# 289 products of zero tiles ahead of the first product, with a stationary operand at eleven distances

## The chip, the cores and the metric

The kernel runs on one core of one Trainium2 chip. What is measured is the device time of one execution in microseconds (us). All times below come from the page of one profiled execution, from answers of its trace, or from the timed runs.

## What is computed

Two transformer blocks run one after the other over 256 tokens of 1024 features, in float32. The first block has a SwiGLU feed-forward part, a mixer made of sparse attention and a gated recurrence, and a second feed-forward part; the second block has two layers with feed-forward parts, forgetting attention or latent attention, and a gated per-layer embedding. The part that the change stands ahead of is the very beginning:

```python
def rms_norm(x, g):
    y = xf * lax.rsqrt(jnp.mean(xf * xf, axis=-1, keepdims=True) + EPS)
    return y * g
def swiglu(x, w_gu, w_down):
    gate, up = jnp.split(x @ w_gu, 2, axis=-1)
    return (jax.nn.silu(gate) * up) @ w_down
h = h + 0.5 * swiglu(rms_norm(h, ffn1_norm), ffn1_w_gu, ffn1_w_down)
```

The output is one array of 256 by 1024. None of the products that the change adds is read by anything, so the output is the same.

## The kernel before

The 256 tokens stand in two tiles of 128 (T = 0 and T = 1), and a generator per tile (`net`, stepped in turns by `run`) walks through the whole network. Every weight matrix is cut into units, and these into pieces of at most 128x512 float32. `load_unit` (L301) brings one piece by DMA from the array `wp` into a buffer `wr` (six buffers, L311), and splits it into a rounded high part (ScalarE, L318) and the remainder (VectorE, L319), both in buffers `w` (42 of them, two to a piece). The activations are split the same way into `xh` and `xl`. A product of full accuracy is then three TensorE products, `mm3` at L343:

```python
mm(out, xh, wh, start=start, stop=False)   # L347
mm(out, xh, wl, start=False, stop=False)   # L348
mm(out, xl, wh, start=False, stop=stop)    # L349
```

The first argument after the output is the stationary operand (128 columns), the second the moving one (up to 512 columns). A piece is thus used by three products for T = 0 and three for T = 1.

`build` loads the first unit (`preload(PRE)`), then the constants and the first x tile; then `run` begins. For each token tile `first_xT` (L501) transposes eight blocks of x (`tr`, L357) into two banks of PSUM named `tr` and `mm`, scales them into `xh` on ScalarE (L507) and into `xl` on VectorE (L509). The statistics of the norm go beside it (L527, L448, L454, L493, L494). `late` (L1443) loads the remaining constants, and `gain` (L426) loads a row of 1024 gains or biases into one of three buffers named `gb` (L435).

The order in which each engine takes its instructions is set by the tile scheduler, in program order with priorities; each engine then takes its queue in order. All DMAs are issued by SyncE's one queue (SP). PSUM has per token tile one bank `mm`, one bank `tr` and two banks `a`, the last of which take turns.

Of the kernel before, what the change touches and what calls it, by code (L numbers as in the profile page):

```python
# [11 lines left out]
FT = mybir.dt.float32  # L12
FR = mybir.dt.float32r
# [5 lines left out]
D = 1024  # L19
S = 256  # L20
P = 128
# [242 lines left out]
class Net:  # L264
# [1143 lines left out]
    def run(self):  # L1408
        gens = [self.net(0), self.net(1)]
        done = [False, False]  # L1410
        send = [None, None]
        cnt = [0, 0]

        def step(T):
            if done[T]:
                return
            self.T = T
            try:
                tag = gens[T].send(send[T])
            except StopIteration:  # L1420
                done[T] = True
                return
            send[T] = None
            if tag is not None:
                send[T] = self.get_unit(cnt[T], tag)
                cnt[T] += 1

        step(0)
        self.nc.sync.dma_start(self.x[1], self.a["x"][P:S, :])
        step(1)  # L1430
        steps = [1, 1]
        while not all(done):
            step(0)
            steps[0] += 1
            lag = min(self.lag_at(cnt[0]), LAG0 + steps[0] // RAMP)
            while steps[0] - steps[1] > (lag if not done[0] else 0) and not done[1]:
                step(1)
                steps[1] += 1
                self.drop_units(cnt[1] - 1)
        assert cnt == [len(self.units)] * 2  # L1440


def late(n, nc, sb, a, vec, ct):  # L1443
    nc.sync.dma_start(ct[:, P:a["const"].shape[1]], a["const"][:, P:])
    lf = n.s2()[:, 0:64 * len(LEVELS)]
    nc.sync.dma_start(lf, a["lvl"])
    n.lvl = sb.tile([P, 64 * len(LEVELS)], U8, name="lvl")
    nc.vector.tensor_copy(n.lvl, lf)
    n.c["cpos"] = sb.tile([P, 2, 16], FT, name="cpos")
    nc.sync.dma_start(n.c["cpos"], a["cpos"])  # L1450
    n.w2 = sb.tile([P, 2, 128], FT, name="w2")
    nc.sync.dma_start(n.w2, a["w2"])
    o, w = vec["fox_b_f_2"]
    nc.sync.dma_start(n.bf, a["vec"][o:o + w].rearrange("(o w) -> o w", o=1).broadcast_to([P, w]))
    for k in ("hgrn_out_norm", "kv_norm_2", "mla_q_norm_2"):
        o, w = vec[k]
        n.small[k] = sb.tile([P, w], FT, name=k)
        nc.sync.dma_start(n.small[k], a["vec"][o:o + w].rearrange("(o w) -> o w", o=1).broadcast_to([P, w]))
    n.fsel = n.misc[:, 0:16]
    nc.scalar.activation(n.fsel, n.c["fsel"], AF.Copy)  # L1460


def build(nc, tc, a, units, offs, coff, vec):
    with tc.tile_pool(name="sb", bufs=1) as sb, tc.tile_pool(name="ps", bufs=1, space=PSUM) as ps:
        n = Net(nc, tc, sb, ps, a, units, offs)
        n.vec = vec
        xs = []
        for T in range(2):
            x = sb.tile([P, D], FT, name=f"x{T}")
            xs.append(x)  # L1470
            if T == 0:
                n.preload(PRE)
                nc0 = a["const"].shape[1]
                ct = sb.tile([P, -(-(nc0 + 24) // 32) * 32], FT, name="const")
                nc.sync.dma_start(ct[:, 0:P], a["const"][:, 0:P])
                nc.sync.dma_start(x, a["x"][0:P, :])
                n.c["g1"] = ct[:, nc0:nc0 + 8]
                n.bf = ct[:, nc0 + 8:nc0 + 24]
                nc.sync.dma_start(n.c["g1"], a["g1"])
                n.x, n.small = xs, {}  # L1480
        for k, (o, w) in coff.items():
            n.c[k] = ct[:, o:o + w]
        n.misc = sb.tile([P, 32], FR, name="misc")
        n.c["mhalf"] = n.misc[:, 16:32].bitcast(FT)
        nc.gpsimd.memset(n.c["mhalf"], -0.5)
        n.late = lambda: late(n, nc, sb, a, vec, ct)
        n.run()
# [43 lines left out]
```

## Time and profile before

| what | us |
|---|---|
| timed runs, median of 2 | 1678.89 (1678.06 to 1679.73) |
| the profiled execution, whole | 1682.29 |
| its span, first to last instruction | 1680.5 |
| TensorE products busy in the span | 1649.4 (98%) |
| VectorE busy | 1110.6 (66%) |
| ScalarE busy | 936.7 (56%) |
| mean granted TensorE clock | 0.995 |

In the views, a line names an instruction by the line of the kernel, the engine, the operation and output<-inputs; PE is TensorE's products, PEld its loads of the stationary operand, DVE is VectorE, ACT ScalarE, POOL GpSimd, and SP the queue that issues DMAs. A product's shown duration includes the time that it takes to drain through the array, so that products overlap in the rows: what a product costs in a stream is the distance from its start to the next one's start, and this is what "pace" means below.

### The profile page before, as it was taken

The page shows a single profiled execution, that of the slowest core. Times are in us where ns is not written, and L with a number is a line of the kernel's source. Part 1 is how long each engine was busy: PE and PEld are TensorE (multiplying, and loading weights), DVE is VectorE, ACT ScalarE, POOL GpSimd, SP SyncE. Part 2 cuts the span into 40 slices and gives each one's busy share as a digit, 9 for nine tenths or more (in the row PEclk, how much of TensorE's full clock was granted, in tenths as well). Part 3 has the DMA queues.
Part 4 walks back from the last instruction along what each step waited for, and adds up shares of the span by engine and source line. Part 5 has one row for each costly group of instructions (what it writes and reads, how often), then busy time and mean ns, then how long its engine had stood idle before and what let it go on. Part 6 is the DMA issues. An engine that isn't in the chain of part 4 may idle for free.

```text
span 1680.5 us, 24829 instructions
## 1 busy us (share of the span) xinstructions
PE 1649.4 (98%) x8010; PEld 1345.9 (80%) x8010; DVE 1110.6 (66%) x2308; ACT 936.7 (56%) x1899; POOL 23.5 (1%) x43
## 2 busy tenths in 40 slices
PE   8999999999999999999999999999999999999997
PEld 6888777778888788877888888778888888888886
DVE  7656666666665766677558666785666865766666
ACT  7555665555555555555555555565555775555553
POOL 0000000000000000000000000000000000000000
PEclk9999999999999999999999999999999999999999
DMA  8855554336565566655436555565665633566552
GB/s 280 269 183 174 173 169 127 101 107 194 188 188 176 175 189 189 186 170 151 146 116 206 186 190 188 176 223 171 201 188 165 211 101 94 188 208 187 189 176 76
DMA packets 160403, 293.00 MB, mean 174 GB/s; under 512 B 18192, under 2 KB 27152, under 8 KB 160272
## 3 DMA queue, kind: packets, MB, share of 16 engines
q1 hardware_dynamic: 160272, 291.41, 55.7%
q8 instruction: 63, 1.03, 0.2%
q14 instruction: 68, 0.56, 0.1%
HBM read 290.29 MB, written 1.05 MB: 173 GB/s over the span
## 4 chain that ended last, share of the span: by engine, by line
PE 87%; DVE 6%; ACT 2%; DMA 2%; issue 2%; POOL 1%; SPq 0%; DVEq 0%; POOLq 0%; ACTq 0%
PE mm L347 16%; PE mm L349 15%; PE mm L348 15%; PE a L347 10%; PE a L348 10%; PE a L349 10%; PE tr L357 4%; DMA wr<-wp 1%; DVE w L319 1%; DVE x L542 1%; PE a L766 1%; ACT w L318 1%; DVE x L559 1%; DVE x L547 1%; PE a L989 1%
## 5 line engine op out<-in xcount | busy, mean ns | idle before, releaser
L319 DVE TENSOR_TENSOR w<-wr,w 128x512 fp32r<-128x512 f32 (+3 forms) x1058 | 702.8, 679 | 355.0 <-ACT w L318 171.0
L318 ACT ACTIVATE w<-wr 128x512 fp32r<-128x512 f32 (+3 forms) x1058 | 648.9, 623 | 395.1 <-PE mm L348 235.3
L347 PE MATMUL mm<-w,xh 128*128 128x512 f32 (+3 forms) x1200 | 477.5, 398 | 0.3 <-DVE s L584 0.3
L349 PE MATMUL mm<-w,xl 128*128 128x512 f32 (+3 forms) x1200 | 465.3, 388 | 0.0
L348 PE MATMUL mm<-w,xh 128*128 128x512 f32 (+3 forms) x1200 | 464.7, 387 | 0.0
L347 PEld LDWEIGHTS mm<-w,xh 128*128 128x128 f32 x1200 | 226.0, 188 | 43.9 <-issue 4.4
L349 PEld LDWEIGHTS mm<-w,xl 128*128 128x128 f32 x1200 | 225.9, 188 | 43.3
L348 PEld LDWEIGHTS mm<-w,xh 128*128 128x128 f32 x1200 | 226.6, 189 | 38.9 <-issue 0.6
L347 PE MATMUL a<-w,s 128*128 128x512 f32 x531 | 208.1, 392 | 0.5 <-ACT s L352 0.5
L348 PE MATMUL a<-w,s 128*128 128x512 f32 x531 | 207.5, 391 | 0.0
L349 PE MATMUL a<-w,s 128*128 128x512 f32 x531 | 207.3, 391 | 0.1
L347 PE MATMUL a<-w,xh 128*128 128x512 f32 (+2 forms) x304 | 119.6, 394 | 0.8 <-ACT xh L352 0.7
L347 PEld LDWEIGHTS a<-w,s 128*128 128x128 f32 x531 | 99.7, 188 | 24.9 <-issue 3.6
L348 PE MATMUL a<-w,xh 128*128 128x512 f32 (+2 forms) x304 | 118.3, 389 | 0.0
L349 PE MATMUL a<-w,xl 128*128 128x512 f32 (+2 forms) x304 | 117.2, 388 | 0.0
L349 PEld LDWEIGHTS a<-w,s 128*128 128x128 f32 x531 | 99.6, 188 | 21.1 <-DVE s L353 0.6
L348 PEld LDWEIGHTS a<-w,s 128*128 128x128 f32 x531 | 99.7, 188 | 19.9
L352 ACT ACTIVATE s<-tr 128x256 fp32r<-128x256 f32 (+2 forms) x137 | 50.6, 371 | 70.8 <-PE tr L357 70.7
L353 DVE TENSOR_TENSOR s<-tr,s 128x256 fp32r<-128x256 f32 (+2 forms) x137 | 56.4, 413 | 47.6 <-ACT s L352 47.3
L357 PE MATMUL tr<-const,s 128*128 128x128 f32 (+1 forms) x436 | 77.5, 274 | 1.9 <-DVE s L471 1.5
L357 PEld LDWEIGHTS tr<-const,s 128*128 128x128 f32 (+1 forms) x436 | 55.9, 140 | 27.6 <-DVE s L471 2.7
L347 PEld LDWEIGHTS a<-w,xh 128*128 128x128 f32 x304 | 57.4, 189 | 14.4 <-ACT xh L352 3.3
(277 smaller groups left out, 1354.9 us busy)
## 6 DMA issues: line engine op xcount, KB each, us to landing
wr<-wp SPq DMA_DIRECT2D x994, 256.0 KB, 2.7
gb<-vec SPq DMA_DIRECT2D x21, 512.0 KB, 4.3
wr<-wp SPq DMA_DIRECT2D x32, 192.0 KB, 2.4
w<-wp SPq DMA_DIRECT2D x16, 256.0 KB, 4.6
wr<-wp SPq DMA_DIRECT2D x16, 160.0 KB, 2.4
wr<-wp SPq DMA_DIRECT2D x8, 168.0 KB, 2.2
wr<-wp SPq DMA_DIRECT2D x8, 140.0 KB, 2.3
x<-x SPq DMA_DIRECT2D x2, 512.0 KB, 5.7
```

The lines of the kernel that those rows point to most:

```text
L318: nc.scalar.activation(hi[:, 0:w], r[:, 0:w], AF.Copy)
L319: nc.vector.tensor_tensor(lo[:, 0:w], r[:, 0:w], hi[:, 0:w].bitcast(FT), op=OP.subtract)
L347: mm(out, xh, wh, start=start, stop=False)
L348: mm(out, xh, wl, start=False, stop=False)
L349: mm(out, xl, wh, start=False, stop=stop)
L352: self.nc.scalar.activation(hi, src, AF.Copy)
L353: self.nc.vector.tensor_tensor(lo, src, hi.bitcast(FT), op=OP.subtract)
L357: self.nc.tensor.transpose(out, src, self.c["ident"][0:n, 0:n])
L542: nc.vector.scalar_tensor_tensor(y[:, cs], y[:, cs], nm, g[:, cs], op0=OP.add, op1=OP.mult)
L547: nc.vector.scalar_tensor_tensor(y[:, cs], y[:, cs], r, b[:, cs], op0=OP.mult, op1=OP.add)
L559: self.nc.vector.scalar_tensor_tensor(x[:, cs], acc, c, x[:, cs], op0=OP.mult, op1=OP.add, accum_out=s)
L766: nc.tensor.matmul(hp[0:2 * nb, 256 * kv:256 * kv + 256], kbs[kv][:, cc].rearrange("p g b -> p (g b)"), u[i][0], start=cc == 0, stop=cc == 15)
```

## The change

A function `probe` is called once, for the first token tile, between the loading of the first weight unit and the loading of the constants. It takes two of the three `gb` buffers, fills both with zeros on VectorE, and issues 289 products on TensorE of which nobody reads the result. The moving operand is always the front of one tile; the stationary operand is 128 columns of the other, starting at byte offset f. There are 24 groups: one of 13 products and 23 of 12. By width: 211 products have 512 columns, 78 have 256. Each group takes one of T = 1's two `a` banks in turn.

```diff
+def probe(nc, n):
+    n.T = 1
+    m, w = n.t("gb", [P, D], 3, FR), n.t("gb", [P, D], 3, FR)
+    for v in (m, w):
+        nc.vector.memset(v.bitcast(FT), 0.0)
+    mm = nc.tensor.matmul
+
+    def run(reps, cols, offs):
+        o = n.pt("a")
+        for i in range(reps):
+            c, f = cols[i % len(cols)], offs[i % len(offs)] // 4
+            mm(o[:, 0:c], w[:, f:f + P], m[:, 0:c], start=True, stop=True)
+
+    run(13, [512], [0])
+    for f in (0, 256, 128, 64, 32, 16, 384, 448, 480, 512, 1024):
+        run(12, [512], [f])
+    run(12, [512], [0, 512, 1024])
+    run(12, [512], [0, 256])
+    run(12, [512], [128, 128, 384])
+    for f in (0, 256, 128, 64):
+        run(12, [256], [f])
+    for f in (0, 256, 128, 64):
+        run(12, [512, 256], [f])
+    run(12, [512, 256], [0, 512])
...
                 n.preload(PRE)
+                probe(nc, n)
                 nc0 = a["const"].shape[1]
```

On TensorE, at the start of the program, the order before begins with the eight transposes of the first x tile (`x_61`), seven products of the first token tile, and the eight transposes of the second (`x_78`):

```order
L357 MATMUL tr_9_83<-const,x_61 128x128 x4
L357 MATMUL mm_10_96<-const,x_61 128x128 x4
L347 MATMUL a_17_121<-w_66,xh_81 128x512
L348 MATMUL a_17_121<-w_67,xh_81 128x512
L349 MATMUL a_17_121<-w_66,xl_82 128x512
L347 MATMUL a_17_121<-w_70,xh_81 128x512
L348 MATMUL a_17_121<-w_71,xh_81 128x512
L349 MATMUL a_17_121<-w_70,xl_82 128x512
L347 MATMUL a_17_121<-w_126,xh_81 128x512
L357 MATMUL tr_32_149<-const,x_78 128x128 x4
L357 MATMUL mm_33_162<-const,x_78 128x128 x4
```

Now the probe's products (L1474) come first. These are its last three rows and what follows them, at the place where the program proper begins:

```order
L1474 MATMUL a_32_378<-gb_74,gb_75 128x256
L1474 MATMUL a_32_378<-gb_74,gb_75 128x512
L1474 MATMUL a_32_378<-gb_74,gb_75 128x256
L357 MATMUL tr_35_400<-const,x_61 128x128 x4
L357 MATMUL mm_36_413<-const,x_61 128x128 x4
L357 MATMUL tr_58_466<-const,x_395 128x128 x4
L357 MATMUL mm_59_479<-const,x_395 128x128 x4
L347 MATMUL a_43_438<-w_66,xh_398 128x512
L348 MATMUL a_43_438<-w_67,xh_398 128x512
L349 MATMUL a_43_438<-w_66,xl_399 128x512
L347 MATMUL a_43_438<-w_70,xh_398 128x512
```

What moved: 289 products stand ahead, and the sixteen transposes of both token tiles now stand together, ahead of the first product.

On ScalarE, at the same place, the order before has the first scaled transposes (L507) behind two pieces of weights (L318) and two statistics:

```order
L318 ACT_TABLE_LOAD
L318 ACTIVATE w_66<-wr_62 128x512
L318 ACTIVATE w_70<-wr_64 128x512
L527 ACTIVATE s_11_109,col_110<-x_61 128x512
L527 ACTIVATE s_13_112,col_113<-x_61 128x512
L507 ACTIVATE xh_81<-tr_9_83,const 128x128 x4
L507 ACTIVATE xh_81<-mm_10_96,const 128x128 x4
```

Now they stand behind 21 pieces of weights, of which these are the last, and the splitting of weights goes on behind them:

```order
L318 ACTIVATE w_673<-wr_667 128x512
L318 ACTIVATE w_693<-wr_689 128x512
L1460 ACTIVATE misc<-const 128x16
L507 ACTIVATE xh_398<-tr_35_400,const 128x128 x4
L507 ACTIVATE xh_398<-mm_36_413,const 128x128 x4
L507 ACTIVATE xh_464<-tr_58_466,const 128x128 x4
L507 ACTIVATE xh_464<-mm_59_479,const 128x128 x4
L318 ACTIVATE w_697<-wr_691 128x512
L318 ACTIVATE w_723<-wr_719 128x512
```

What moved: 19 pieces more are split ahead of the first L507, and VectorE's order (L319, L509) has the same shift.

On SP, the first `gb` row (`gb_717`, what each waits for in brackets) stood before among the weights, and waited for no engine:

```order
L311 DMA wr_673<-wp 128x512 [waits DMAHW6_49,DVE_49]
L1458 DMA kv_norm_712<-vec 128x256
L1458 DMA mla_q_norm_714<-vec 128x384
L435 DMA gb_717<-vec 128x1024 [waits DMAHW7_49]
L311 DMA wr_719<-wp 128x512 [waits DMAHW0_49,DVE_49]
```

Now three such rows stand together, behind 27 pieces of weights and ahead of the 28th (`wr_776`):

```order
L1458 DMA mla_q_norm_1031<-vec 128x384 [waits DMAHW5_49]
L435 DMA gb_1034<-vec 128x1024 [waits DMAHW6_49]
L435 DMA gb_2327<-vec 128x1024 [waits DMAHW7_49,PE_49]
L435 DMA gb_4233<-vec 128x1024 [waits DMAHW0_49]
L311 DMA wr_776<-wp 128x512 [waits DMAHW1_49,DVE_49]
L311 DMA wr_804<-wp 128x512 [waits DMAHW2_49,DVE_49]
```

What moved: the second of them, into a buffer that the probe uses, now waits for TensorE, and everything behind it on SP waits with it.

Beyond the first 140 rows of each engine the order is that of before.

## Rows read from the trace of the kernel before

**Rows 1.** The page: span, busy time of the engines (share, instructions).

```profile
span 1680.5 us, 24829 instructions
...
PE 1649.4 (98%) x8010; PEld 1345.9 (80%) x8010; DVE 1110.6 (66%) x2308; ACT 936.7 (56%) x1899; POOL 23.5 (1%) x43
```

**Rows 2.** Waits of TensorE: who, for what: us in total, times, longest.

```profile
PE tr L357 <- DMA x<-x: 7.4, 1, 7.4
PE tr L357 <- DVE x L547: 4.9, 12, 0.9
```

**Rows 3.** Timeline, TensorE's last product: start us, us, engine, line, output<-inputs.

```profile
1671.03 0.39 PE L349 MATMUL mm<-w,s 128*128 128x512 f32 x1
```

**Rows 4.** Timeline of the start, as above, with [idle before <-releaser].

```profile
0.73 1.28 ACT L318 ACT_TABLE_LOAD   x1 [0.73 <-PEq L1523]
...
4.21 1.31 DVE L319 TENSOR_TENSOR w<-wr,w 128x512 fp32r<-128x512 f32 x2 [4.21 <-ACT w L318]
...
7.40 1.08 PE L357 MATMUL tr<-const,x 128*128 128x128 f32 x4 [7.40 <-DMA x<-x]
...
8.53 1.14 ACT L507 ACTIVATE xh<-tr,const 128x128 fp32r<-128x128 f32 x4
...
10.74 0.63 PE L347 MATMUL a<-w,xh 128*128 128x512 f32 x1
...
11.16 0.43 PE L348 MATMUL a<-w,xh 128*128 128x512 f32 x1
...
11.67 0.40 PE L347 MATMUL a<-w,xh 128*128 128x512 f32 x1
...
11.90 0.60 PE L357 MATMUL tr<-const,x 128*128 128x128 f32 x4
...
12.34 0.60 PE L357 MATMUL mm<-const,x 128*128 128x128 f32 x4
...
12.70 0.48 PE L348 MATMUL a<-w,xh 128*128 128x512 f32 x1
```

**Rows 5.** Timeline of TensorE, two places in a stream of 128x512 products.

```profile
72.45 0.39 PE L349 MATMUL mm<-w,xl 128*128 128x512 f32 x1
...
81.52 0.39 PE L347 MATMUL a<-w,s 128*128 128x512 f32 x1
81.74 0.39 PE L348 MATMUL a<-w,s 128*128 128x512 f32 x1
81.97 0.39 PE L349 MATMUL a<-w,s 128*128 128x512 f32 x1
...
82.42 0.39 PE L348 MATMUL a<-w,s 128*128 128x512 f32 x1
```

**Rows 6.** Stretches: us, busy (instructions) by engine PE, PEld, DVE, ACT, POOL, clock, DMA.

```profile
72.45:82.43 9.98, 9.98 (x46) 8.26 (x45) 6.62 (x12) 5.88 (x10) 0.00 (x0) 1.00 0.69 214
...
338.90:345.70 6.80, 6.80 (x30) 6.39 (x30) 1.07 (x3) 1.01 (x6) 0.00 (x0) 0.50 0.00 0
...
779.20:782.70 3.50, 3.50 (x11) 2.69 (x10) 1.52 (x7) 1.43 (x7) 0.00 (x0) 0.51 0.11 22
```

**Rows 7.** Timeline of TensorE, a stream of 128x256 products, 17 rows left out.

```profile
1298.77 0.28 PE L1198 MATMUL mm<-keep,w 128*128 128x256 f32 x1
...
1300.92 0.28 PE L1198 MATMUL a<-keep,w 128*128 128x256 f32 x1
```

**Rows 8.** Groups by line: xcount | busy us, mean ns | idle before, releasers.

```profile
L817 POOL MEMSET s<- 128x512 f32 x4 | 2.0, 527 | 21.6 <-PE a L832 21.6
```

**Rows 9.** The page's groups: splitting of weights, and a load of the stationary operand.

```profile
L319 DVE TENSOR_TENSOR w<-wr,w 128x512 fp32r<-128x512 f32 (+3 forms) x1058 | 702.8, 679 | 355.0 <-ACT w L318 171.0
L318 ACT ACTIVATE w<-wr 128x512 fp32r<-128x512 f32 (+3 forms) x1058 | 648.9, 623 | 395.1 <-PE mm L348 235.3
...
L347 PEld LDWEIGHTS mm<-w,xh 128*128 128x128 f32 x1200 | 226.0, 188 | 43.9 <-issue 4.4
```

**Rows 10.** The page's DMA issues: xcount, KB each, median us to landing.

```profile
wr<-wp SPq DMA_DIRECT2D x994, 256.0 KB, 2.7
```

## The prediction

> **What bounds the kernel now.** I read the page's busy times first: TensorE's products fill 1649.4 of 1680.5 us, 31.1 us less than the span, and no other engine comes near [rows 1]. So work that is put on TensorE's queue lengthens the run unless it falls into one of TensorE's gaps. The waits of TensorE say where the gaps are: the largest is one of 7.4 us at the very start, for the first x tile; behind it come 4.9 us in twelve pieces for the layer norms, the longest 0.9 us [rows 2]. The last product starts at 1671.03 and ends at 1671.42, so 9.1 us at the end hold none [rows 3]. That leaves 31.1 - 7.4 - 9.1 = 14.6 us of idle time in the middle. Only the first gap lies where the new products stand. Third, I read the timeline of the first 13 us, because it shows what happens in that gap and how slowly TensorE runs just after it [rows 4].
>
> **The pace of a product.** TensorE's rows overlap, so I count starts. From 72.45 to 82.42 us there are 45 starts, 44 distances (46 products touch the stretch, one of them was already in flight): 9.97 / 44 = 0.2266 us for each 128x512 product at clock 1.00 [rows 5, 6]. The pace does not depend on whether the stationary operand was used by the product before: L347 to L348, with the same one, is 0.22, and L348 to L349, with another one, 0.23 [rows 5]. For 128x256 there are 18 distances from 1298.77 to 1300.92: 2.15 / 18 = 0.119 us [rows 7]. The two differ by 0.107 us for 256 columns. At this rate 512 columns alone would take 0.214, so about 0.013 us a product comes on top of its columns. A 128x128 transpose in a run takes 0.11 us: 0.44 us from 11.90 to 12.34 for four [rows 4].
>
> The Trainium skill (TensorE: Matmul & The Clock Gate, "Back-to-back issue gap") gives N / 2.4 + 2.5 ns for an isolated product, 0.216 us at 512 columns, and about 0.131 us as a sustained spacing in streams of load and product. The row here lies above both. With 0.216 the sum below would be 2.2 us smaller; with 0.131 it would be smaller by nearly 20 us, which is a rival below.
>
> **When the probe can start.** It needs two zeroed tiles of 128x1024. VectorE has nothing to do until 4.21, and the engines take their first instruction at 0.73 [rows 4]. No row shows a memset on VectorE. GpSimd's of 128x512 takes 0.527 us [rows 8], so I take twice that, 1.05 us, for each of the two: 0.73 + 2.1 = 2.85, and 2.9 with a hand-over. If VectorE needed what it needs for a subtraction of 128x512 (0.679 us) [rows 9], they would end at 3.45; if nothing, at 0.73. So the start lies between 0.8 and 3.6. The memsets end before 4.21 and delay nothing on VectorE.
>
> **How long it lasts.** The first products run at the slow clock. Before, TensorE began at 7.40; the distance at 10.74 was still 0.42 us [rows 4], and from 11.67 to 11.90 it was 0.23, so the slow stretch was about 3.8 us. I take 3.8 us for the probe as well: 3.8 / 0.42 = 9 products. Then 202 of 512 columns at 0.2266 make 45.8 us and 78 of 256 at 0.119 make 9.3 us. The probe ends at 2.9 + 3.8 + 45.8 + 9.3 = 61.8 us. The first transpose, which started at 7.40, starts there: **54.4 us later**. The 4.5 us from 2.9 to 7.40 are the part of the probe that lies in the old gap.
>
> **What comes back.** The slow stretch has then been paid by the probe. Before, sixteen transposes and seven products took 12.70 - 7.40 = 5.3 us, part of it the slow clock and part a wait for the first `xh` and `xl` [rows 4]. Now sixteen transposes take 16 x 0.11 = 1.76 and seven products 7 x 0.2266 = 1.59, together 3.4: **1.9 us back**. For this the first `xl` must not be late. Four transposes are done 0.7 us after the first starts; four L507 take 1.14 [rows 4], so the first L509 starts some 1.9 us after the probe's end and the first `xl` is there at 2.2. The third product, which needs it, comes at 1.76 + 2 x 0.23 = 2.2: just in time, at worst 0.3 us lost.
>
> **What is queued behind the new waits.** ScalarE's and VectorE's first L507 and L509 now stand behind 21 pieces of weights, but these are split during the probe: at 0.679 us each [rows 9] VectorE needs 14 us, and the probe lasts 59. All 42 `w` buffers are then full, and SP has loaded six pieces more. At the probe's end TensorE holds 21 pieces of six products each: 21 x 6 x 0.2266 = 28.6 us of work, while ScalarE is back at splitting after sixteen L507, 16 x 0.29 = 4.6 us. From then on ScalarE and VectorE need 0.62 and 0.68 us for a piece that feeds TensorE for 1.36 [rows 9], so weights do not run short. SP's new wait (the second `gb` load for the end of the probe) holds up the 28th piece and all behind it; that piece needs a `wr` buffer that only comes free after the probe anyway. Hidden, then, by 28.6 us of stock; without the stock the first piece would cost its landing of 2.7 us [rows 10] once, not each piece.
>
> **The sum.** 54.4 - 1.9 = 52.5 us. Against the profiled execution, 1682.29 + 52.5 = 1734.8; it ran 3.4 us longer than the timed median, so for timed runs 1678.89 + 52.5 = **1731.4 us**, 3.1% more. A measurement of this kernel can tell about 2% from no change, that is 33.6 us.
>
> **The bounds.** Pace: 0.214 and 0.107 (columns alone) give 2.7 + 0.9 = 3.6 us less; 0.236, by 0.01 a product slower than the stream, 2.1 more. Start: 2.1 less or 0.7 more. A slow stretch twice as long as before: 1.8 more. In two later stretches the granted clock was 0.50, for 6.8 and 3.5 us [rows 6]; shifted against the gaps they may vanish or repeat, half of 10.3 us either way. Together about 10 us each way: 1721 to 1742.
>
> **Rivals.**
>
> *Loads that are no longer hidden.* A load of the stationary operand lasts 0.188 us [rows 9] and the pace of 0.2266 shows it almost wholly under the product before. The probe puts the stationary tile at distances that the stream may not have. If a load fell out from under its product at some distance, that product would cost 0.214 + 0.188 = 0.40, 0.175 more, and a group of 12 would cost 2.1 us more. Five such groups give 1742, all 24 give 1731.4 + 50.6 = 1782. For it speaks that the groups differ in nothing but this; against it that the stream's loads are hidden with several kinds of tile. The Trainium skill (TensorE: Matmul & The Clock Gate, "Step-by-step: what each phase is for") says that TensorE reads the two operands through two independent ports, so that a load does not take bandwidth from the running product; by that all groups have one pace, and it speaks against this rival. No row of before shows it either way. Chance of more than 1746: 5%.
>
> *A repeated operand issues faster, and the run is within 2%.* Each group repeats one stationary tile and one moving tile. If a 512-column product in it went at the pace of a 256-column one, 0.119, the probe would be over at 2.9 + 289 x 0.119 = 37.3, the shift 37.3 - 7.4 - 1.9 = 28, and the time 1707. It decides from a mean pace of (33.6 + 1.9 + 7.4 - 2.9) / 289 = 0.138 downwards. Against it: in the stream the second use of the same stationary tile is no faster [rows 5]. The skill's sustained 0.131 us would be of this kind. Chance 2%.
>
> *The lead is paid back.* TensorE starts the program proper with 21 pieces instead of two in stock. If that removed all 14.6 us of idle time in the middle, 52.5 - 14.6 gives 1716.8, still slower. Against it: the waits are for x and the norms, none for weights [rows 2], and ScalarE's largest wait is for TensorE, not the other way [rows 9]. Chance 3%.
>
> *Zeros do not raise the clock.* Between 338.9 and 345.7 the clock was 0.50 (1.2 of 2.4 GHz) with TensorE busy all the time [rows 6], so busy rows alone do not hold it. If zero tiles never raised it, 211 x 0.42 + 78 x 0.21 = 105 us, nothing would come back, and the time would be 1678.9 + 2.9 + 105 - 7.4 = 1779. Against it: the probe's products are back to back and of the form that raised it from 7.40 on. Chance 3%.
>
> **How the numbers follow.** The forecast, 1721 to 1742, has 82%; slower in part by unhidden loads up to 1746, 3%; the rivals 5, 2, 3 and 3%, and 2% for what I have not seen. The range from 1720 to 1746 leaves out 15%. Faster by over 2% needs the probe to save time, for which nothing speaks: 1%. Within 2%: the fast rival and some of the unseen, 3%. Slower: 96%.
>
> **What would show it.** In the new profile the first L1474 row should stand near 2.9 us and the first L357 near 62. Steps of starts within the probe: 0.42 for some 4 us, then 0.227 and 0.119 in every group; a group at another pace tells of the distance. The first product after the transposes should come 1.8 us behind the first L357, and the products behind it at 0.227 with no wait for `w`. The prediction is wrong if the end of the probe lies outside 51 to 73 us, or if what follows the transposes lasts other than 1680.5 - 12.7 us by more than 6.

## The result and the profile after

The changed kernel takes 1731.76 us (median of 1731.42 and 1732.09), 52.9 us more than before. The ratio is 1.0308, with a 95% interval from 1.0287 to 1.0330. The forecast was 1731.4, in a range from 1720 to 1746.

The page of the changed kernel's profiled execution (1731.42 us, span 1729.7; first fence line the span, second the busy times) answers to [rows 1]: TensorE is busy for 54.6 us more in a span that is 49.2 us longer, and the other engines' work is the same within 4 us.

```profile
span 1729.7 us, 25412 instructions
...
PE 1704.0 (99%) x8299; PEld 1392.4 (81%) x8299; DVE 1114.6 (64%) x2310; ACT 939.2 (54%) x1899; POOL 23.1 (1%) x43
```

The timeline of the start (start us, us, engine, line, output<-inputs, then in brackets idle time and what ended it) answers to [rows 4]. Equal rows are merged, so the row of L1474 holds the first 32 products of the probe:

```profile
1.02 0.91 DVE L1467 MEMSET gb<- 128x1024 f32 x1 [1.02 <-PEq L1550]
...
2.09 0.91 DVE L1467 MEMSET gb<- 128x1024 f32 x1 [0.16 <-issue]
...
3.06 9.23 PE L1474 MATMUL a<-gb,gb 128*128 128x512 f32 x32 [3.06 <-DVE gb L1467]
```

And the end of the probe, in the same view:

```profile
62.73 0.60 PE L357 MATMUL tr<-const,x 128*128 128x128 f32 x4
62.92 0.81 SPq L435 DMA_DIRECT2D gb<-vec  x2
...
63.36 1.14 ACT L507 ACTIVATE xh<-tr,const 128x128 fp32r<-128x128 f32 x4 [30.13 <-PE tr L357]
...
64.39 0.48 PE L347 MATMUL a<-w,xh 128*128 128x512 f32 x1
...
64.94 0.19 PEld L349 LDWEIGHTS a<-w,xl 128*128 128x128 f32 x1 [0.28 <-DVE xl L509]
...
66.21 0.39 PE L348 MATMUL a<-w,xh 128*128 128x512 f32 x1
```

The reader is to see four things. The probe starts at 3.06. The first transpose, at 7.40 before, starts at 62.73. ScalarE had been idle for 30 us when the transposes came: all the weights that the buffers hold had been split. SP's two held-up `gb` loads go out at 62.92, right behind the probe, and nobody waits for them.

Paces within the probe come from stretches that begin and end with a product's start. The columns are: stretch, its length, PE busy with the number of products that touch it (one to three of them were in flight at its start), granted clock, DMA share and GB/s:

```profile
3.06:6.64 3.58, 3.58 (x9) 1.00 0.92 291
13.27:32.81 19.54, 19.54 (x86) 1.00 0.89 285
32.81:43.69 10.88, 10.88 (x50) 1.00 0.18 62
47.92:49.36 1.44, 1.44 (x15) 1.00 0.00 0
...
50.78:52.15 1.37, 1.37 (x14) 1.00 0.00 0
```

The first eight distances take 3.58 us, the second to the eighth of them 0.427 each: this is the slow clock, though the first row shows 1.00, because the trace has no entry of the clock before 6.63, where it is recorded as full. The 48 products from 32.81 on, at distances that are multiples of 256 bytes, step at 10.88 / 48 = 0.2267 us. The 84 from 13.27 on, at seven distances that are not, step at 19.54 / 84 = 0.2326. The last two rows are groups of twelve products of 256 columns: 1.44 / 12 = 0.120 at a distance of 256 bytes, 1.37 / 12 = 0.114 at 64. So at 256 columns the multiple of 256 is not the faster distance.

| step | forecast, us | measured, us |
|---|---|---|
| probe starts | 2.9 | 3.06 |
| slow stretch | 3.8 | 3.6 |
| 512 columns, each | 0.2266 | 0.2267 or 0.2326 |
| 256 columns, each | 0.119 | 0.114 to 0.120 |
| probe ends | 61.8 | 62.73 |
| first transpose later by | 54.4 | 55.3 |
| sixteen transposes, seven products | 3.4 (5.3 before) | 3.48 |
| timed median later by | 52.5 | 52.9 |

Behind its first 38 instructions TensorE's own order is that of before, so that one product can be followed through the runs. The product that starts at 72.45 in [rows 5] stands here in the changed kernel and in `before2`, a second profile of the kernel before:

```profile
125.33 0.39 PE L349 MATMUL mm<-w,xl 128*128 128x512 f32 x1
```

```profile
72.30 0.39 PE L349 MATMUL mm<-w,xl 128*128 128x512 f32 x1
```

The product is 52.9 us later than in the first profile of before and 53.0 later than in the second. Against the second, every later product up to some 750 us keeps this distance within 0.1 us.

### The profile page after: what moved, and what is told of

Read it like the earlier page. It is cut to its first block, busy times and chain, and to the rows that moved or that the text cites. A ratio compares the mean times of both kernels' runs of the same rounds, so it can differ in the third digit from the quotient of the medians.

```text
span 1729.7 us, 25412 instructions
## 1 busy us (share of the span) xinstructions
PE 1704.0 (99%) x8299; PEld 1392.4 (81%) x8299; DVE 1114.6 (64%) x2310; ACT 939.2 (54%) x1899; POOL 23.1 (1%) x43
## 3 DMA queue, kind: packets, MB, share of 16 engines
q1 hardware_dynamic: 160272, 291.41, 54.4%
HBM read 290.29 MB, written 1.05 MB: 168 GB/s over the span
## 4 chain that ended last, share of the span: by engine, by line
PE 91%; DVE 5%; issue 1%; ACT 1%; POOL 1%; DMA 0%; DVEq 0%; POOLq 0%; ACTq 0%
PE mm L347 16%; PE mm L349 15%; PE mm L348 15%; PE a L347 10%; PE a L348 10%; PE a L349 10%; PE tr L357 4%; PE a L1474 3%; DVE x L542 1%; PE a L766 1%; DVE w L319 1%; DVE x L559 1%; DVE x L547 1%; PE a L857 1%; PE a L1281 1%
## 5 line engine op out<-in xcount | busy, mean ns | idle before, releaser
L319 DVE TENSOR_TENSOR w<-wr,w 128x512 fp32r<-128x512 f32 (+3 forms) x1058 | 703.9, 679 | 358.8 <-ACT w L318 162.5
L318 ACT ACTIVATE w<-wr 128x512 fp32r<-128x512 f32 (+3 forms) x1058 | 649.9, 622 | 399.9 <-PE mm L348 243.2
```

The costliest lines, as they stand in the source:

```text
L318: nc.scalar.activation(hi[:, 0:w], r[:, 0:w], AF.Copy)
L319: nc.vector.tensor_tensor(lo[:, 0:w], r[:, 0:w], hi[:, 0:w].bitcast(FT), op=OP.subtract)
```

## Experiments

The timed comparisons have runs of the kernel before on the same chip beside them, 1679.2 to 1679.3 in the median.

**Is the cost the products' own?** `double` runs the list of groups twice; the first of the 24 repeated calls is shown.

```diff
     run(12, [512, 256], [0, 512])
+    run(13, [512], [0])
...
```

> The probe's 289 products twice over, 578. By the theory that the time is the products' own pace beyond the gap: the second half runs at full clock throughout, 59.7 us less eight slow products at 0.2 us too much, 58.0 us: 1731.8 + 58.0 = 1789.8 us (1787 to 1793). Rival 'part of the 52.9 us is a fixed cost of the shift' (start-up, order, clock): the second half adds clearly less or more than 58, for example 52.9 - 4.3 + 10 us.

It took 1789.72 us (ratio 1.0653, 1.0636 to 1.0669): 58.0 us more than with one list, and 58.0 were forecast. In the traces, the product of 72.45 us stands at 183.65, 58.3 us behind its place with one list, where the clock rose 0.9 us sooner. What one list costs less than the second, 58.0 - 52.9 = 5.1 us, is mostly what the old gap and the slow clock account for: 4.3 from 3.06 to 7.40, 1.8 that comes back, less 1.6 for eight slow products, 4.5 in all. A fixed cost of more than about 1 us is not left over.

**Does the old gap hide the beginning?** `late_start` makes the stationary tile a copy of x and calls the probe behind the load of x, so that the probe must wait for it.

```diff
-    for v in (m, w):
-        nc.vector.memset(v.bitcast(FT), 0.0)
+    nc.vector.memset(m.bitcast(FT), 0.0)
+    nc.vector.tensor_copy(w, x)
...
                 nc.sync.dma_start(x, a["x"][0:P, :])
+                probe(nc, n, x)
```

> The whole probe, but its stationary tile is a copy of the first x tile instead of zeros, so that it can't start before x has landed (about 7.2 us) and been copied (1.1 to 1.4 us). Theory 'the old gap hides the probe's first 4.3 us': it starts near 8.5 instead of 3.06 us, 5.4 us later; the scheduler puts the first four transposes ahead of it, 0.4 us that then lie in the gap: 1731.8 + 5.0 = 1736.8 (1735 to 1739). Rival 'what stands in the gap makes no difference to the end': 1731.8. Since the stationary data are no longer zeros, the paces by distance (0.227 and 0.231 to 0.234) also say whether zeros mattered.

It took 1736.16 us (1.0338, 1.0317 to 1.0360), 4.4 us more than the changed kernel in the median; its four runs lie between 1734.4 and 1740.5, so the traces tell more. The timeline of its start has the copy done sooner than I had assumed, in 0.69 us:

```profile
7.09 0.69 DVE L1467 CAST gb<-x 128x1024 fp32r<-128x1024 f32 x1 [1.56 <-DMA x<-x]
7.21 1.09 PE L357 MATMUL tr<-const,x 128*128 128x128 f32 x4 [7.21 <-DMA x<-x]
7.94 1.63 PE L1474 MATMUL a<-gb,gb 128*128 128x512 f32 x3
```

The product that starts at 125.33 in the changed kernel:

```profile
128.95 0.39 PE L349 MATMUL mm<-w,xl 128*128 128x512 f32 x1
```

The probe starts at 7.94, 4.9 us later than at 3.06. Four transposes lie ahead of it (0.4 us less behind it), and its clock rose after 2.1 us instead of 3.6, which saves half of 1.5 us: 4.9 - 0.4 - 0.75 = 3.7, and the product is 3.6 us later. The theory of the gap holds; the rival asked for no difference. The paces were those of zeros.

**Is a probe that fits into the gap free?** `warm11` keeps the first 11 products.

```diff
-    run(13, [512], [0])
-    for f in (0, 256, 128, 64, 32, 16, 384, 448, 480, 512, 1024):
...
+    run(11, [512], [0])
```

> Only the first 11 products of the probe stand, all at distance 0. By the theory that the old gap hides what lies in it: they start at 3.06 us, run at the slow clock for 3.6 us and end at 7.35, before the x tile lands at 7.4, so they cost nothing; the four products from 10.15 to 11.67 then run at full clock, 0.6 us less: 1678.3 us. Rival 'whatever stands on TensorE's queue lengthens the run': 11 products at 0.3 to 0.43 us, 1682 to 1684. Rival 'all of the slow clock comes back': 1.8 us less, 1677.1.

It took 1683.88 us (1.0019, 1.0008 to 1.0031), 5.6 us more than my theory's 1678.3 and, by the interval, 1.3 to 5.2 us more than before. The products started at 3.06 as expected, but in the profiled execution the clock rose only at 9.27, so all of them were slow and the first transpose followed at 7.92, 0.5 us later than before. And TensorE waited later. These are its waits from 8 to 56 us (who, for what: us in total, times, longest):

```profile
PE mm L347 <- DVE s L584: 2.2, 2, 1.2
PE a L347 <- ACT w L318: 0.6, 1, 0.6
PE a L349 <- DVE xl L509: 0.4, 1, 0.4
PE a L348 <- DVE w L319: 0.3, 1, 0.3
```

Before, the first of them was 0.3 us and the others, but for `xl`, were not there. The scheduler's order had changed: the second token tile's statistics (L527) stand ahead of the next pieces of weights, and the load of the constants stands later on SP, so that ScalarE waits 2.9 us at L1460 for it. `w2` separates the order from the products: two products, the same order.

> The probe with 2 products instead of 11; every engine's order is that of the 11-product kernel, which ran 3 us longer than before. Theory 'the order, not the products': any product at this place lets the scheduler move the load of the constants and the statistics of the second token tile, weights come late in the first 56 us, and 2 products cost as much as 11: 1682 to 1685. Rival 'the products themselves': 2 products at 0.4 us end long before x lands, so the time is that of before, 1679 to 1680.

It took 1681.29 us (1.0015, 1.0003 to 1.0028), between the two theories and with an interval that overlaps that of 11 products. That it is slower than before at all speaks for the order; the timed runs do not resolve the size. Its profile shows the wait at L584 again, 1.4 us. `warm11b` was the 11-product kernel a second time:

> The 11-product kernel once more, for a second profile. Theory 'the order makes weights come late': TensorE waits again near 12 to 13 us and near 46 and 56 us, and stands 2 to 3 us behind before at 56 us. Rival 'one disturbed execution': it does not.

Its profile has that wait once, at 0.9 us, and the same waits of 0.6, 0.4 and 0.3 us. So it was no single disturbed execution, but it was smaller. The product of 72.45 us in `warm11`, `warm11b` and `w2`, one fence each:

```profile
76.29 0.39 PE L349 MATMUL mm<-w,xl 128*128 128x512 f32 x1
```

```profile
74.84 0.39 PE L349 MATMUL mm<-w,xl 128*128 128x512 f32 x1
```

```profile
74.88 0.39 PE L349 MATMUL mm<-w,xl 128*128 128x512 f32 x1
```

It is 3.8, 2.4 and 2.4 us later than before. Two products cost as much as eleven in the second profile, though in `w2` they held nothing up: its first transpose started at 7.09. So this is the cost of the order.

`w11const` moved the constants' load forward again:

```diff
         self.nc.sync.dma_start(self.x[1], self.a["x"][P:S, :])
+        self.nc.sync.dma_start(self.ct[:, P:self.a["const"].shape[1]], self.a["const"][:, P:])
...
-    nc.sync.dma_start(ct[:, P:a["const"].shape[1]], a["const"][:, P:])
```

> The 11-product probe, with the load of the remaining constants put on SP right behind the second x tile again (before: two pieces of weights later; in the 11-product kernel six pieces later). Theory: ScalarE's wait of 2.9 us for the constants at 18.7 us goes, and with it TensorE's two waits of 1.4 and 1.1 us near 46 and 56 us: about 2.5 us less than with 11 products alone, 1680 to 1682; the two waits near 12 to 13 us, behind the statistics, stay. Rival 'the constants do not matter': as with 11 products alone, 1684.

> The 11-product kernel with the constants' load moved forward, once more, for a second profile: in the first one the waits near 46 and 56 us were gone, but the timed runs were not shorter. Theory 'the constants were the cause of these two waits': they are gone again. Rival 'chance': one of them is back.

In both profiles the waits at L584 are gone, with ScalarE's wait at L1460, and the rest is as it was, but for one of 0.6 us for x in the second; the first one's list, for 8 to 56 us, is complete:

```profile
PE a L347 <- ACT w L318: 0.6, 1, 0.6
PE a L349 <- DVE xl L509: 0.4, 1, 0.4
PE a L348 <- DVE w L319: 0.3, 1, 0.3
```

And the product of 72.45 us, in the first:

```profile
72.92 0.39 PE L349 MATMUL mm<-w,xl 128*128 128x512 f32 x1
```

It is 0.5 us late instead of 2.4 or 3.8 (2.0 in the second profile, with 3.4 us at half the clock ahead of it). So the constants' place caused those waits. The timed runs do not show the gain: 1682.65 us (1.0016, 1.0005 to 1.0027), 12 runs from 1677.6 to 1684.7. The second profile took 1688.88 us, mostly because the clock was at 0.50 in four stretches within it (3.4 us at 12.9, 6.8 at 340.6, 6.8 at 361 and 3.4 at 784). What makes its timed runs long in the median is open in the main: their granted clock was 0.9967 in the mean, that of the 29 runs of before beside them 0.9972, which by an estimate (the difference times 1680 us) is less than 1 of the 2.7 us between the means. No short probe was faster than the kernel before, so there is no better version here.

**Why the profiles differ by more than the sum.** From the eighth product on, the changed kernel's profiled execution was 4.3 us shorter than that of before. `before2` is the kernel before, unchanged.

> The kernel before, unchanged, once more, for a second profile. After the probe, the changed kernel's profiled run is 4.3 us shorter than the profiled run of before had been from the same product on, most of it at two stretches where the clock was at 0.50 before. Theory 'the slow stretches fall differently from execution to execution': the stretches at 338.9 (6.8 us) and 779.2 (3.5 us) are missing, shorter or elsewhere, and the span differs from 1680.5 by half of what they differ, 1676 to 1680. Rival 'the change moved them': both stand where they stood, and the span is 1680.5 within 0.5.

Its span was 1677.9 us, 2.6 less than in the first profile. The stretches of before at clock 0.50 are in [rows 6]; these are the same places in the second execution (columns as above):

```profile
339.30:342.75 3.45, 3.45 (x18) 0.51 0.00 0
779.40:782.90 3.50, 3.50 (x19) 1.00 0.25 77
```

One stretch is half as long, the other is not there. The changed kernel has one too, of 3.4 us, at the same products (392.3 less the shift of some 53 us is 339.3):

```profile
392.30:395.70 3.40, 3.40 (x18) 0.51 0.02 5
```

So `before2` has the same fall from 10.2 to 3.4 us at half the clock as the changed kernel has, and it gained 1.2 us at each of the two places, 2.4 in all. Another 0.5 us is a wait that the first profile of before has and `before2` has not (the first two rows are of before, the third is of `before2`):

```profile
51.45 0.39 PE L349 MATMUL mm<-w,xl 128*128 128x512 f32 x1
52.09 0.47 PE L347 MATMUL mm<-w,xh 128*128 128x512 f32 x1 [0.26 <-DVE s L584]
```

```profile
52.04 0.39 PE L347 MATMUL mm<-w,xh 128*128 128x512 f32 x1
```

The changed kernel has no such wait either. As the unchanged kernel can be without it, it is not shown to be the change's doing. That leaves some 1.4 of the 4.3 us, which `before2` did not gain; about 1 us of it lies between 742 and 802 us of before, and its cause is open. The slow stretches come from execution to execution, not from the change. Both stand where TensorE had been busy with narrow products and short waits: for 5.67 of the 7.0 us ahead of the first, for 5.71 of the 6.8 us ahead of the second.

**Which distances matter, and what else does.** `scan` replaces the groups.

```diff
+    for mo, so in ((0, 0), (128, 0), (0, 128), (128, 128), (64, 0), (64, 64), (256, 0), (256, 256), (32, 160)):
+        run(12, m, mo, 512, w, so)
+    for k, so in ((64, 0), (32, 0), (64, 128), (32, 128)):
+        run(12, m, 0, 512, w, so, k)
...
+    for c in (480, 448, 384, 320, 256, 192, 128):
+        for so in (0, 32, 64, 96, 128):
+            run(12, m, 0, c, w, so)
...
+    run(12, v, 0, 512, w, 0)
```

> The probe is replaced by groups of 12 products (24 in the first) that vary one thing at a time: the start of the moving operand, the start and the width of the stationary one, the width of the moving one, and the data (ones instead of zeros). In the changed kernel's trace 512-column products step at 0.227 us at distances that are multiples of 256 bytes and at 0.231 to 0.234 at the others. Theory 'relative distance': moving and stationary both shifted by 128 or by 64 bytes step at 0.227 again, moving alone shifted by 128 at 0.232. Rival 'alignment of the stationary operand alone': moving shifted by 128 with the stationary at 0 stays at 0.227, and both shifted by 128 step at 0.232. On what lies above the columns' own 0.213 us: if it is the loading of the stationary operand, 64 columns of it step at about 0.220 and 32 at 0.217; if it is a fixed cost of a product, they stay at 0.227. On the data: ones step like zeros if data do not matter (0.227 at a distance of 2048 bytes, 0.232 at 2176).

Stretches of twelve starts each, in order: neither operand shifted, the moving one by 128 bytes, the stationary one by 128, both by 128; then 64 stationary columns, a distance of 2048 bytes, four groups of 128 moving columns (48 starts), and ones instead of zeros:

```profile
10.32:13.04 2.72, 2.72 (x14) 1.00 0.91 291
13.04:15.83 2.79, 2.79 (x13) 1.00 0.84 264
15.83:18.63 2.80, 2.80 (x14) 1.00 0.89 299
18.63:21.37 2.74, 2.74 (x14) 1.00 0.82 294
35.13:37.89 2.76, 2.76 (x13) 1.00 0.00 0
85.13:87.85 2.72, 2.72 (x13) 1.00 0.00 0
146.07:151.40 5.33, 5.33 (x51) 1.00 0.00 0
161.09:163.82 2.73, 2.73 (x14) 1.00 0.07 29
```

It is the relative distance: shifting either operand costs 0.006 us a product (2.80 against 2.72 for twelve), shifting both costs nothing once the group has settled (2.74, the first three starts carry the rest). 2048 bytes is as good as 0, and so were 256 and 768; of all others tried between 4 and 508, most stepped at 0.232 to 0.234; 192, 448, 496 and 508 did at 0.227 to 0.230, and 8 at 0.230. It is no smooth rule: 224 and 480, nearer to a multiple of 256 than 192 and 448, stepped at 0.233. The sign matters: 64 more is slower than 64 less. Narrower stationary operands did not help (2.76), so the theory that the load's width sets the 0.013 us above the columns is wrong. Ones step like zeros. At 128 columns the pace is 5.33 / 48 = 0.111 us.

All this is for 512 columns. These are twelve starts each of 480 columns at distances of 0, 32 and 128 bytes, and of 320 columns at 0 and 128:

```profile
87.85:90.44 2.59, 2.59 (x13) 1.00 0.00 0
90.44:93.01 2.57, 2.57 (x14) 1.00 0.00 0
98.21:100.84 2.63, 2.63 (x14) 1.00 0.00 0
123.48:125.24 1.76, 1.76 (x13) 1.00 0.00 0
130.52:132.28 1.76, 1.76 (x14) 1.00 0.03 9
```

At 480 columns a distance of 32 is a little faster than 0 (0.214 against 0.216); at 320 the distance does nothing (0.147 at both).

`scan2` looked for these 0.013 us.

```diff
+    run(12, 512, [W], [M], 2)
+    run(12, 512, [W], [M], 1, True)
...
+    run(12, 512, [w[0:64, 0:P]], [m[0:64, 0:512]])
+    run(12, 512, [b[:, 0:P]], [b[:, 512:1024]])
+    run(12, 512, [b[:, 64:64 + P]], [b[:, 512:1024]])
...
+    run(12, 256, [b[:, 0:P]], [b[:, 512:768]])
+    run(12, 128, [b[:, 0:P]], [b[:, 512:640]])
```

> The probe is replaced by groups of 12 products at distance 0 that look for the 0.013 us by which a 512-column product (0.2266) exceeds its columns (0.2134): two banks of PSUM in turn, one accumulating chain, two moving tiles in turn, four stationary tiles, 64 rows instead of 128, and 2-byte operands (bfloat16) at three widths. Theory 'it is a cost of reading 4-byte operands at full rate': 2-byte operands step nearer to 0.2134 (about 0.216), the others stay at 0.2266. Rival 'it is a cost of writing one bank of PSUM again': two banks in turn step faster. Rival 'a fixed cost of a product': nothing changes it.

Two banks, an accumulating chain, two moving tiles and four stationary tiles all settle at 0.227. 2-byte operands do not, at either distance tried: these are twelve starts of 512 columns shifted by 128 bytes, and twelve of 256 columns:

```profile
28.29:30.88 2.59, 2.59 (x14) 1.00 0.99 338
33.25:34.56 1.31, 1.31 (x13) 1.00 0.12 40
```

2.59 / 12 = 0.216 and 1.31 / 12 = 0.109. So the excess, and the effect of distance with it, belongs to 4-byte operands. What causes it stays open.

**Does distance matter outside the probe?** `pad128` and `pad256` have no probe, but an unused tile between the weights and what is allocated behind them.

```diff
-        return self.t("col", [P, n], 24)
+        return self.t("col", [P, n], 20)
...
                 n.preload(PRE)
+                pad = sb.tile([P, 32], FT, name="pad")
+                nc.vector.memset(pad, 0.0)
```

> No probe. The kernel before with an unused tile of 128 bytes per partition between the weights and all later tiles (two to four small column buffers fewer make room); the order on every engine is that of before. 5793 products of 512 columns now have the stationary operand 128 bytes off the moving one, modulo 256, instead of 0. By the probe's paces (0.2266 at 0, 0.232 to 0.234 at 128) the time grows by 5793 x 5.4 to 7.2 ns = 31 to 42 us: 1710 to 1721. Rival 'distance matters in the probe alone, because there one stationary tile is repeated': 1679 to 1680.

> The control: the same with an unused tile of 256 bytes, which leaves the distance at 0 modulo 256. Theory 'distance modulo 256': 1679 to 1680, as before. Rival 'the fewer column buffers or the shift itself cost': the same as with 128 bytes.

With 128 bytes it took 1701.75 us (1.0136, 1.0119 to 1.0153), with 256 bytes 1678.62 (0.9999, 0.9990 to 1.0009). The order is the same in both. So distance matters in the kernel's own stream, and a shift by 256 cost nothing that the runs resolve. Five distances in the stream of the first, and five in that of the second:

```profile
72.60 0.40 PE L347 MATMUL mm<-w,xh 128*128 128x512 f32 x1
72.84 0.40 PE L348 MATMUL mm<-w,xh 128*128 128x512 f32 x1
...
73.76 0.39 PE L349 MATMUL mm<-w,xl 128*128 128x512 f32 x1
```

```profile
71.66 0.39 PE L349 MATMUL mm<-w,xl 128*128 128x512 f32 x1
71.89 0.39 PE L347 MATMUL mm<-w,xh 128*128 128x512 f32 x1
...
72.79 0.39 PE L348 MATMUL mm<-w,xh 128*128 128x512 f32 x1
```

1.16 / 5 = 0.232 against 1.13 / 5 = 0.226. The direction was right and the size too large: 22.5 us instead of 31 to 42. I had taken the settled paces. The stream settles anew behind every break (in the changed kernel the second to the seventh product behind the transposes step at 0.229 to 0.239, but for the one that waits for `xl`), so that its mean pace is 0.228 even at distance 0, and 0.232 at 128: 4.4 ns for some 5500 products, 24 us. Counted over both traces, only the products of 512 columns are slower; those of 384 and 320 columns step within 0.001 us of what they do with 256 bytes.

## Why the prediction was right, point by point

**The bound.** It said that work on TensorE lengthens the run except in the first gap. `double` shows the first half (58.0 us for 58.0 us of products), `late_start` the second (3.6 us in the traces for a start that is 3.7 us later, net).

**The start.** Forecast 2.9, measured 3.06: each memset took 0.91 instead of 1.05 us, and VectorE began at 1.02 instead of 0.73.

**The slow stretch.** 3.6 us for a forecast of 3.8. This was luck in part: from one execution to another the clock rose 2.1 us (`late_start`, behind four transposes), 3.6, 4.5 (`double`), 5.7 (`scan2`) and 6.2 us (`warm11`) after the probe's start.

**The pace.** At 512 columns right where the distance is a multiple of 256 bytes, 2.6% too low at the seven others; at 256 columns right but for a distance of 64, where 0.119 was 4% too high. Groups that alternate the two widths took 0.350 to 0.354 us a pair at every distance, instead of 0.346. This is the one step that failed in kind: the prediction said that every group would step at 0.227 and 0.119, and put a deviation down only as a load that falls out from under its product, 2.1 us a group. No load fell out from under its product (a step would have been 0.40); the steps are 0.006 us longer, for a reason that no run shows. The probe takes 59.67 us instead of 58.9, about 0.8 more, which is why the sum hardly noticed.

**What comes back.** 5.30 - 3.48 = 1.8 us for a forecast of 1.9. The first `xl` came 0.1 us late, as the prediction allowed.

**The queues.** No product behind the probe waited for weights; ScalarE idle for 30 us shows that the stock was full. The rival of the paid-back lead got nothing that is shown to be its own: the wait at 52.09 is missing in `before2` as well, and against `before2` the shift stays at 53.0 us up to some 750 us. `warm11` shows the other side: without the stock, a changed order at this place does cost a few microseconds. The prediction's sum for the full probe was safe from this because the stock covers it.

**The rivals.** A repeated operand does not issue faster (0.2267). Zeros raise the clock like other data.

**The sum.** 55.3 - 1.8 = 53.5 us, 1.0 more than the forecast of 52.5: the start, the length of the probe and what comes back were each a little off, and all in one direction. What the forecast had not foreseen took some of it back: in the first profile of before the wait at 52.09 costs 0.5 us, in the second x lands at 7.73 instead of 7.40, which leaves the 52.9 and 53.0 us seen at the product of 72.45. Both come with the execution, so that the medians differ by 52.9, only 0.4 from the forecast, is luck in part. The profiled executions differ by 49.1, mostly because that of before had 6.8 us more at half the clock, and the wait: a sum made against it alone would have seemed 3.4 us off.

## What to carry to other kernels

Work added to an engine that is 98% busy costs its own pace in the stream, counted from start to start, less only what falls into a gap that is there already; read the gap from the waits and the start of the new work from what it waits for. Work that fits into a gap is still not free where a scheduler sets the order: two products at the start moved other engines' instructions, and in the trace the program ran 2.4 us late though no transpose had waited for the two. Where 4-byte products have 512 columns, keep the stationary and the moving tiles a multiple of 256 bytes apart; 128 bytes of unused memory cost this kernel 1.4%. Do not carry this to narrower products without a measurement: at 320 columns the distance did nothing here, at 480 and 256 another one was faster.

## What the runs showed of the hardware that I had not expected

In settled groups a 128x512 product of 4-byte operands stepped at 0.2267 us when the stationary operand was a multiple of 256 bytes away from the moving one, at 0.227 to 0.230 at 192, 448, 496 and 508 bytes, and at 0.232 to 0.234 at most other distances; 2-byte operands stepped at 0.216 at both distances tried. Among the 4-byte products of the kernel's own stream, only those of 512 columns were slower at 128 bytes. The Trainium skill (TensorE: Matmul & The Clock Gate, "Step-by-step: what each phase is for") has the two operands read through independent ports, so that a load takes nothing from the running product. For 2-byte operands the runs agree; a pace of 4-byte products that depends on where the two operands lie to each other does not fit it, and the measurement decides, though no run shows what the two reads do to each other. The Trainium skill (TensorE: Matmul & The Clock Gate, "Back-to-back issue gap") gives N / 2.4 + 2.5 ns; 0.216 and 0.109 us for 2-byte operands agree with it, 0.2267 for 4-byte operands is 11 ns more. The sustained 0.131 us for 512 columns that the Trainium skill gives there appears in no run.

Settled groups of 4-byte products with 128 or 192 columns did not step faster than 0.111 us, at any of five distances; with 2-byte operands and 128 columns 0.056 was reached.

The granted clock fell to 0.50 (1.2 of 2.4 GHz) for 3.4 or 6.8 us (10.2 once, in `scan`) at places where TensorE runs narrow products and short waits, in some executions and not in others: 10.2 us in all in one profile of the kernel before, 3.4 in the next, none while TensorE ran in those of `w2` and `w11const`. In 29 timed runs the kernel before ranged from 1676.7 to 1685.2 us. Time and mean granted clock go together there: the five runs above 1681 us had a clock of 0.993 to 0.995, all others 0.997 to 0.999.
